# Five matrix products of a hybrid SSD and attention layer as seven block products for eight, the gates moved ahead of the scan

## The chip, the cores and the metric

One core of a Trainium2 chip runs the whole layer. The metric is the device time of one execution in microseconds: the kernel before took 2068.98 us (median of three runs, 2068.79 to 2068.99).

The engines are named as in the profile: PE (TensorE, matrix products; PEld its weight loads), DVE (VectorE), ACT (ScalarE), POOL (GpSimd), SP (the engine that issues most transfers). Each works through its own queue in order.

## The reference

A layer for 512 tokens of width 2048, in float32: a state space branch (SSD) and a latent attention branch side by side, gated, summed, projected, and normalised. Cut to what matters:

```python
h = rmsnorm(x, norm_w)
u = h @ w_in
z_ssm, xbc, dt_f, dt_b, q_a, kv_a, z_attn, g_ssm, g_attn = jnp.split(u, cuts, axis=-1)
xbc = silu(dwconv(xbc))                       # 4 taps over time
y = ssd_scan(...) + flip(ssd_scan(flip ...)) + d_skip * xs   # 32 heads of 64, 4 groups, chunks of 128
y = y.reshape(b, s, D_SSM) * silu(z_ssm)
y = rmsnorm(per group of 512)
q  = rmsnorm(q_a) @ w_uq ; kv = rmsnorm(kv_a) @ w_ukv        # 16 heads, rotary part of 64
o = bidir_attention(...) * silu(z_attn)
merged = sigmoid(g_ssm) * (y @ w_proj_ssm) + sigmoid(g_attn) * (o @ w_proj_attn)
x = x + merged @ w_out ; out = rmsnorm(x)
```

The products `h @ w_in` for z_ssm, g_ssm and g_attn and the two projections are each 512 x 2048 x 2048: the five products of the title.

## The kernel before, in words

**Products.** float32 operands are split into a high part rounded to PE's fp32r format and a low rest, and a product is three matmuls per 128 rows of depth (high x high, high x low, low x high). h is held transposed in `h_h` and `h_l` (16 tiles of depth by 512 tokens). Weights arrive from SP as chunks of 128x1024 (512 KB) into `wraw` (three buffers); ACT copies the chunk to `wh` (L153), DVE subtracts to `wl` (L154), and a chunk then feeds 24 matmuls: one result tile is 128 features by 512 tokens, two chunks, 48 matmuls in one PSUM bank (L158 to L160).

**Order of the work.** PE's instructions stand as the program writes them. A queue, `Fill`, holds generators of matmuls of weight products, and `gap()` takes a fixed number of them out between steps of the scan or of attention, so that PE has work while DVE, ACT and POOL prepare the next step. The other engines' orders are set by the scheduler at build time, by program order with a head start for weight loads and splits (`AHEAD = 60` instructions).

**Stages.** h is built; the tile of dt follows; then four groups of the scan (`ssd_group`). A group computes its six tiles of x, B and C (convolution rows L387 to L389, SiLU), transposes them (L424), and runs 18 pauses of 40 matmuls (4 tiles of z, 11 tiles of the gates silu(z_attn), sigmoid(g_ssm), sigmoid(g_attn), which go to DRAM). Between the pauses: weighted inputs `xw` on POOL (L483) and their split (L486, L487), local states `loc`, state updates, off-diagonal products; `yo` = D skip (L516, POOL); then for each of 4 chunks and 2 halves the decay sums (scan, L548), E (L551), G (L556 to L559) and the diagonal product `yb` (L569). z times y is normalised per group (sums of squares on PE, `rp`, L318) and stored, features by tokens. After the scan q and kv are compressed and rotary tables made, with the last four gate tiles as PE's cover; then 16 heads of attention (softmax on DVE and ACT; transposes of the probabilities L845), with the next heads' products and, in the last heads, the first projection's as filling. At the end the two projections (`wps` on y, `wpa` on o, 16 result tiles each), the gating and sum, and the output product (L997 to L999).

Of the kernel before, what the change touches and what calls it, by code (L numbers as in the profile page):

```python
# [18 lines left out]
P = 128  # L19
D = 2048  # L20
# [17 lines left out]
T_Z = T_XBC + 24  # L38
T_QA = T_Z + 16
T_KVA = T_QA + 6  # L40
T_ZA = T_KVA + 4
T_GS = T_ZA + 16
T_GA = T_GS + 16
N_TILES = T_GA + 16

# [28 lines left out]
Y_AHEAD = 4  # L74


def build(tc, a):
# [36 lines left out]
    zs_d = [dr.tile([P, SEQ], F32, name=f"zs_d{i}") for i in range(16)]  # L114
    gs_d = [dr.tile([P, SEQ], F32, name=f"gs_d{i}") for i in range(16)]
    ga_d = [dr.tile([P, SEQ], F32, name=f"ga_d{i}") for i in range(16)]
    y_d = [dr.tile([P, SEQ], F32, name=f"y_d{i}") for i in range(16)]
    o_d = [dr.tile([P, SEQ], F32, name=f"o_d{i}") for i in range(16)]
# [123 lines left out]
    sp = open_pool("sp", reuse_waits="tile")  # L242
    krp = open_pool("krp", side="right", reuse_waits="tile")
    kraw = krp.tile([P, SEQ], F32, name="kraw")
    dtp = in_gemm(T_DT, "dtp")
    kr_d = dr.tile([64, SEQ], F32, name="kr_d")
    act.copy(kraw[64:128, :], dtp[64:128, :])
    act.dma_start(kr_d, kraw[64:128, :])
    close_pool("krp")

    scn = sp.tile([P, 2 * SEQ], F32, name="scn")
    act.dma_start(scn, a["scn"])
    scan_f, scan_b = scn[:, :SEQ], scn[:, SEQ:]
    dsk = sp.tile([P, P], F32, name="dsk")[:, :NH]
    act.dma_start(dsk, a["dsk"].broadcast_to([P, NH]))

    dtT = sp.tile([P, TT, 64], F32, name="dtT")
    daT = sp.tile([P, TT, 64], F32, name="daT")
    da_d = dr.tile([64, SEQ], F32, name="da_d")
    ex = sp.tile([P, 2, 2, TT, NH], F32, name="ex")  # L260
    wst = sp.tile([P, 2, TT, NH], F32, name="wst")
    dec = sp.tile([P, TT, 64], F32, name="dec")


    dv_ = gp.tile([P, SEQ], F32, tag="st", bufs=3, name="dv_")
    dt64 = gp.tile([P, SEQ], F32, tag="st", bufs=3, name="dt64")
    act.activation(dv_[0:64, :], dtp[0:64, :], AF.Identity, bias=vec[0:64, V_DTB:V_DTB + 1])

    def dt_make(new):
# [23 lines left out]
        act.dma_start(da_d[NH:64, :], pl[NH:64, :])  # L293

# [57 lines left out]

    def gemm_steps(out, chunks, xh, xl):
# [10 lines left out]
    def gate_gen(tile_i, fn, dst):  # L364
        p_ = mm("gp")
        yield from gemm_steps(p_, win(tile_i), h_h, h_l)
        g_ = gp.tile([P, SEQ], F32, tag="st", bufs=3, name="gate")
        act.activation(g_, p_, fn)
        act.dma_start(dst, g_)

    gates = deque()
    for t0, fn, dst in ((T_ZA, AF.Silu, zs_d), (T_GS, AF.Sigmoid, gs_d), (T_GA, AF.Sigmoid, ga_d)):
        for i in range(16):
            gates.append((t0 + i, fn, dst[i]))
# [6 lines left out]

    def conv_silu(pst, ch, o):

        w = lambda k: vec[:, V_CW + ch * CW + k:V_CW + ch * CW + k + 1]
        acc = tmp2("cacc")
        act.activation(acc, pst, AF.Identity, bias=vec[:, V_CB + ch:V_CB + ch + 1], scale=w(2))
        dve.scalar_tensor_tensor(acc[:, 2:SEQ], pst[:, 0:SEQ - 2], w(0), acc[:, 2:SEQ], ALU.mult, ALU.add)  # L387
        dve.scalar_tensor_tensor(acc[:, 1:SEQ], pst[:, 0:SEQ - 1], w(1), acc[:, 1:SEQ], ALU.mult, ALU.add)
        dve.scalar_tensor_tensor(acc[:, 0:SEQ - 1], pst[:, 1:SEQ], w(3), acc[:, 0:SEQ - 1], ALU.mult, ALU.add)  # L389
        act.activation(o, acc, AF.Silu)  # L390
        return o
# [11 lines left out]
    def z_gen(g, ct, zs):  # L403
        p_ = mm("zp")
        yield from gemm_steps(p_, win(T_Z + 4 * g + ct), h_h, h_l)
        act.activation(zs[:, ct, :], p_, AF.Silu)

    pending = []

    def ssd_group(g):  # L410
# [27 lines left out]
        conv_silu(in_gemm(T_XBC + 6 * g + 4), 16 + g, BT)  # L438
        if g:
            pending.pop(0)()  # L440
        if g == 0:
            ahead[0] = AHEAD
            dt_make(tmp2)
        conv_silu(in_gemm(T_XBC + 6 * g + 5), 20 + g, CT)
        post_b()
        act.copy(c_h, CT)
        pool.tensor_sub(c_l, CT, c_h.bitcast(F32))
        prev = None
        for ct in range(4):
            xs = conv_silu(in_gemm(T_XBC + 6 * g + ct), 4 * g + ct, tmp2("xs"))  # L450
            if prev:
                prev()
            prev = post_x(ct, xs)
            if g == 0 and ct == 2:
                dt_turn()
            if g == 0 and ct == 3:
                dt_sums()

        zs = sw.tile([P, 4, SEQ], F32, tag="zs", name="zs")
        for ct in range(4):  # L460
            fill.add(("z", g, ct), z_gen(g, ct, zs))
        for _ in range(11):
            fill.add("gate", gate_gen(*gates.popleft()))
# [673 lines left out]
```

## Time and profile before

| what | number |
|---|---|
| median of the runs | 2068.98 us |
| the profiled execution | 2069.04 us, span 2067.3 us |
| start until the first transposes | 13 us |
| scan, four groups | about 55 to 1050 us, 249 us a group |
| compression, rotary tables | about 1050 to 1200 us |
| attention | about 1200 to 1515 us |
| projections | about 1515 to 1890 us |
| output product | about 1890 to 2067 us |

How to read the page: the header gives the span of the profiled execution; part 1 the busy time of each engine; part 2 the same in 40 slices in tenths, with the granted clock of PE and the transfer rates; part 4 the chain of work that ended last, by engine and by line; part 5 groups of instructions with busy time, mean duration of one and the idle time ahead of them with its releaser; part 6 the transfers with their median time to landing. The timeline lists single instructions: start, duration, engine, line, operation. The windows view gives for a stretch its length and the busy time of each engine in it.

### The profile page before, as it was taken

What the parts mean: (1) busy time and instruction counts of PE and PEld (TensorE: products, weight loads), DVE (VectorE), ACT (ScalarE), POOL (GpSimd) and SP (SyncE); (2) the same over time, 40 slices, a digit from 0 to 9 for tenths busy, and PEclk for the clock granted to TensorE, in tenths of its full rate; (3) what the DMA queues carried; (4) which work ended last, traced back from release to release, by engine and by line L of the source; (5) the groups of instructions that cost most, each with busy time, mean ns of one, the idle gap of its engine ahead of it and who ended that gap; (6) DMA issues with size and microseconds to landing.
All of it is one profiled execution on the core that took longest, in us unless ns stands there. A gap on an engine that the chain in (4) does not pass through costs nothing.

```text
span 2067.3 us, 24135 instructions
## 1 busy us (share of the span) xinstructions
PE 2035.6 (98%) x9498; PEld 1681.3 (81%) x9498; DVE 1122.7 (54%) x1531; ACT 791.2 (38%) x1103; POOL 189.8 (9%) x139
## 2 busy tenths in 40 slices
PE   6999999999999999999999999999999999999998
PEld 5888888888888888888788888888878888888886
DVE  4646755567545675447674657677663334343342
ACT  5433443334433354334433434444442222222232
POOL 1031000311003100111100000000011010000110
PEclk9999999999999999999999999999999999999999
DMA  5423443245332453224433333323345444335342
GB/s 186 124 82 116 155 131 112 87 128 162 121 108 83 148 153 122 92 90 150 138 122 103 105 119 88 102 81 98 102 123 168 145 150 134 122 119 182 104 141 81
DMA packets 116881, 252.16 MB, mean 122 GB/s; under 512 B 11168, under 2 KB 44064, under 8 KB 116768
## 3 DMA queue, kind: packets, MB, share of 16 engines
q1 hardware_dynamic: 101088, 222.33, 34.7%
q10 hardware_dynamic: 15680, 28.29, 3.7%
q8 instruction: 74, 1.21, 0.2%
q14 instruction: 39, 0.32, 0.0%
HBM read 220.96 MB, written 25.43 MB: 119 GB/s over the span
## 4 chain that ended last, share of the span: by engine, by line
PE 98%; DVE 1%; DMA 1%; ACT 0%; issue 0%; ACTq 0%
PE gp L158 8%; PE gp L159 8%; PE gp L160 8%; PE mm L160 6%; PE mm L158 6%; PE mm L159 6%; PE zp L158 3%; PE zp L160 3%; PE f L997 3%; PE zp L159 3%; PE f L998 3%; PE f L999 3%; PE pb L845 1%; PE qp L160 1%; PE qp L158 1%; PE qp L159 1%
## 5 line engine op out<-in xcount | busy, mean ns | idle before, releaser
L154 DVE TENSOR_TENSOR wl<-wraw,wh 128x1024 fp32r<-128x1024 f32 (+2 forms) x332 | 401.7, 1210 | 571.5 <-ACT wh L153 549.2
L153 ACT CAST wh<-wraw 128x1024 fp32r<-128x1024 f32 (+1 forms) x336 | 341.3, 1017 | 828.8 <-PE gp L159 214.1
L158 PE MATMUL gp<-h_h,wh 128*128 128x512 f32 x768 | 302.4, 394 | 0.0
L159 PE MATMUL gp<-h_l,wh 128*128 128x512 f32 x768 | 299.2, 390 | 0.0
L160 PE MATMUL gp<-h_h,wl 128*128 128x512 f32 x768 | 299.1, 390 | 0.0
L158 PE MATMUL mm<-h_h,wh 128*128 128x512 f32 x544 | 215.2, 396 | 0.0
L160 PE MATMUL mm<-h_h,wl 128*128 128x512 f32 x544 | 212.0, 390 | 0.0
L159 PE MATMUL mm<-h_l,wh 128*128 128x512 f32 x544 | 211.8, 389 | 0.0
L160 PEld LDWEIGHTS gp<-h_h,wl 128*128 128x128 f32 x768 | 144.2, 188 | 30.3
L158 PEld LDWEIGHTS gp<-h_h,wh 128*128 128x128 f32 x768 | 144.3, 188 | 29.9 <-issue 0.9
L159 PEld LDWEIGHTS gp<-h_l,wh 128*128 128x128 f32 x768 | 144.3, 188 | 29.3 <-issue 0.2
L159 PEld LDWEIGHTS mm<-h_l,wh 128*128 128x128 f32 x544 | 102.2, 188 | 22.0 <-issue 1.2
L158 PEld LDWEIGHTS mm<-h_h,wh 128*128 128x128 f32 x544 | 102.2, 188 | 21.8 <-issue 1.2
L160 PEld LDWEIGHTS mm<-h_h,wl 128*128 128x128 f32 x544 | 102.1, 188 | 21.5
L158 PE MATMUL zp<-h_h,wh 128*128 128x512 f32 x256 | 100.5, 392 | 0.0
L160 PE MATMUL zp<-h_h,wl 128*128 128x512 f32 x256 | 99.7, 389 | 0.0
L159 PE MATMUL zp<-h_l,wh 128*128 128x512 f32 x256 | 99.6, 389 | 0.0
L548 DVE TENSOR_TENSOR_SCAN sum<-da,scn 128x512 f32<-128x512 f32 x64 | 83.4, 1318 | 0.0
L997 PE MATMUL f<-wh,mh 128*128 128x512 f32 x208 | 80.9, 389 | 0.0
L998 PE MATMUL f<-wl,mh 128*128 128x512 f32 x208 | 80.9, 389 | 0.0
L999 PE MATMUL f<-wh,ml 128*128 128x512 f32 x208 | 80.9, 389 | 0.0
L835 ACT ACTIVATE pr<-s,nm 128x512 f32<-128x512 f32 x64 | 44.1, 689 | 79.7 <-DVE nm L833 78.2
(3625 smaller groups left out, 3715.0 us busy)
## 6 DMA issues: line engine op xcount, KB each, us to landing
wraw<-wi SPq DMA_DIRECT2D x198, 512.0 KB, 3.5
da<-da_d SPq DMA_DIRECT2D x64, 256.0 KB, 3.8
wraw<-wps SPq DMA_DIRECT2D x32, 512.0 KB, 3.5
wraw<-wpa SPq DMA_DIRECT2D x32, 512.0 KB, 3.7
wraw<-wo SPq DMA_DIRECT2D x32, 512.0 KB, 3.5
wraw<-wun SPq DMA_DIRECT2D x16, 384.0 KB, 3.0
xt<-x SPq DMA_DIRECT2D x8, 512.0 KB, 8.5
zs_d<-gate ACTq DMA_DIRECT2D x16, 256.0 KB, 2.9
```

What stands on the lines that cost most here:

```text
L153: act.copy(h, raw)
L154: (dve if ahead[0] else pool).tensor_sub(l, raw, h.bitcast(F32))
L158: pe.matmul(out, wh, xh, start=start, stop=False)
L159: pe.matmul(out, wh, xl, start=False, stop=False)
L160: pe.matmul(out, wl, xh, start=False, stop=stop)
L548: dve.tensor_tensor_scan(sums[dd], flat(da), mask, 0.0, ALU.add, ALU.mult)
L835: act.activation(pr, s, AF.Exp, bias=nm, scale=SCALE, accum_out=sm_)
L845: pe.transpose(tp[:, k * P:(k + 1) * P], prs[t][:, k * P:(k + 1) * P], ident)
L997: pe.matmul(acc, mh[:, tk], h[k], start=(kk == 0), stop=False)
L998: pe.matmul(acc, mh[:, tk], l[k], start=False, stop=False)
L999: pe.matmul(acc, ml[:, tk], h[k], start=False, stop=(kk == KT - 1))
```

## The change

**Seven for eight.** Each of the five products is cut into two halves of its columns (`cp`). A half is a 2 x 2 block product: tokens in two halves of 256, depth in two halves of 1024, columns in two blocks of 512. Instead of eight block products, seven are made of sums of blocks (Winograd's form, P1 to P7), each of 48 matmuls of 512 columns into two PSUM banks; the weights are now the moving operand, the result stands tokens by features, and a weight chunk feeds 12 matmuls instead of 24.

**Sums.** Of weight blocks: a transfer issued by POOL that adds a second block from DRAM into the chunk in place (`w_more`), and two DVE additions per chunk (`t2`, `t4`). Of result blocks: ACT evicts, DVE adds. Of h's blocks: DVE (`h_sums`), during the first xBC tiles; the block x21 of h is overwritten with S3 while the gates run and loaded back behind them. Of y's and o's blocks: transfers from DRAM to DRAM on POOL (copies and adding ones), then loads and splits like weights.

**Order.** Only group 0's xBC tiles come first; then z, sigmoid(g_ssm), sigmoid(g_attn) in full, to DRAM; then the scan, whose 18 pauses a group are filled with the next group's xBC tiles, the q and kv compression and silu(z_attn): 480 matmuls in the first three groups (27 or 26 to a pause), 576 in the last (32). y is normalised per 128 tokens on DVE and ACT (`y_norm`), transposed (`y_turn`) and stored. The normalisation of the compressed q and kv moves behind the scan, with 96 matmuls of silu(z_attn) left. In the last head three products of the first projection (`wps.head()`, 144 matmuls) are the filling; the operand blocks of y for the rest are loaded when the heads' memory is closed. `wpa`'s results get the first projection's by an adding transfer, and are transposed (64 more transposes) for the output product.

```diff
+    def w_more(t, w, cp, kh, cb, m, ahead_=AHEAD):
+        with tc.high_priority(offset=ahead_):
+            pool.dma_start(t, a[w][cp, kh, cb, m], accum_op=ALU.add)
...
+    def product(name, op, chunk, extra=None, pre=None):
+        bs = banks(name)
+        for m in range(4):
+            raw = chunk(m)
+            h, l = w_split(raw)
+            if extra:
+                extra(m, raw)
...
+            for i in range(2):
+                for jj in range(2):
+                    j = 2 * m + jj
+                    xh, xl = op(0, j, i), op(1, j, i)
+                    wh, wl = (t[:, jj * 512:(jj + 1) * 512] for t in (h, l))
+                    pe.matmul(bs[i], xh, wh, start=(j == 0), stop=False)
+                    pe.matmul(bs[i], xh, wl, start=False, stop=False)
+                    pe.matmul(bs[i], xl, wh, start=False, stop=(j == 7))
...
+                p1 = evict((yield from product("P1", self.op("x11"), c1, lambda m, raw: w_more(raw, w, cp, 0, 1, m))), "p1")
...
+            p5 = evict((yield from product("P5", self.op("S1"), c5, t2)), "p5")
...
+            A = yield from product("P6", self.op("S2"), lambda m: X[m],
...
+                yield from self.second(cp, p1, lambda i: p1[i], t4)
...
+            B = yield from product("P3", self.op("S4"), lambda m: Y[m], lambda m, raw: w_more(raw, w, cp, 0, 1, m),
...
+            A = yield from product("P7", self.op("S3"), lambda m: Y[m], None, self.pre(2, 2 * cp + 1))
...
+            A = yield from product("P4", self.op("x22"), lambda m: X[m], None, self.pre(2, 2 * cp))
...
+        left = [(10 * 48, 10 * 48, 10 * 48, 12 * 48)[g], 18]
...
+                y = sw.tile([P, SEQ], F32, tag="yz", bufs=2, name="y")
+                dve.tensor_add(y, yo[:, c], yb)
+                y_norm(c, g, y)
...
+    close_pool("at")
+    xb = cols = open_pool("xb", side="right", reuse_waits="tile")
+    for w in ("S1", "S2", "S4", "S3", "x22"):
+        y_ops.load(w)
+        y_ops.split(w, slot(w))
     fill.all()
...
+    run(wps.pair(0, True))
+    run(wps.pair(1, True))
+    sets[0] = list(range(4))
+    run(wpa.pair(0))
+    run(wpa.pair(1))
```

**Three places in the order.** On DVE at the first weights, before: the splits of the dt tile and group 0 stand among the rows of dt and of the convolution (`cacc`).

```order
L154 TENSOR_TENSOR wl<-wraw,wh 128x1024
L283 SCALAR_TENSOR_TENSOR pl<-pl,u 64x512
L284 SCALAR_TENSOR_TENSOR pl<-pl,e 64x512
L286 SCALAR_TENSOR_TENSOR dt_435<-pl,dv__434 64x512
L288 TENSOR_SCALAR da_518<-dt_435,small 64x512
L292 TENSOR_TENSOR pl<-dt_435,small 32x512
L387 SCALAR_TENSOR_TENSOR cacc<-mm,vec,cacc 128x510
```

Now, up to DVE's seventh weight split (the last row here), the sums of h's blocks (L651 to L671) and the splits of the sums (L421) stand with them:

```order
L666 TENSOR_TENSOR s_688<-x_686,x_678 128x1024
L282 SCALAR_TENSOR_TENSOR pl<-pl,e 64x512
L668 TENSOR_TENSOR x_686<-x_680,x_686 128x1024
L284 SCALAR_TENSOR_TENSOR dt_481<-pl,dv__480 64x512
L651 TENSOR_TENSOR x_694<-h_h,h_l 128x1024
L286 TENSOR_SCALAR da_489<-dt_481,small 64x512
L290 TENSOR_TENSOR pl<-dt_481,small 32x512
L377 SCALAR_TENSOR_TENSOR cacc<-xbc,vec,cacc 128x510
L421 TENSOR_TENSOR S_517<-x_686,S_517 128x1024
L378 SCALAR_TENSOR_TENSOR cacc<-xbc,vec,cacc 128x511
L162 TENSOR_TENSOR wl<-wraw,wh 128x1024
```

From DVE's first weight split to its seventh stand 26 operations of 128x1024, the splits included.

On POOL at the beginning of group 1 of the scan, before: behind the last G2 of group 0 come C's low part, two weighted inputs and the D skip.

```order
L557 TENSOR_TENSOR G_1950<-dtT,cbb 128x512
L557 TENSOR_TENSOR G_2036<-dtT,cbb 128x512
L557 TENSOR_TENSOR G_2124<-dtT,cbb 128x512
L447 TENSOR_TENSOR c_l<-CT,c_h 128x512
L483 TENSOR_TENSOR xw<-xT,wst 128x512 x2
L516 TENSOR_TENSOR yo<-xT,dsk 128x512 x4
```

Now, in group 2 (in groups 0 and 1 the same without the transfers):

```order
L832 TENSOR_TENSOR c_l<-CT,c_h 128x512
L1213 DMA yn_S_205<-yn_x_203 16x16384
L898 TENSOR_TENSOR yo<-xT,dsk 128x512 x4
L1216 DMA yn_S_207<-yn_x_203 512x512
L865 TENSOR_TENSOR xw<-xT,wst 128x512 x4
```

The D skip and the copies and sums of y's blocks went ahead of the first weighted input.

On DVE behind the last head's product with the values, before: `og` is the gated output of head 15, then operand splits of y alternate with the splits of weights.

```order
L859 TENSOR_TENSOR og<-op,zt 128x512
L867 TENSOR_TENSOR y11l<-y11st,y11h 128x512
L154 TENSOR_TENSOR wl<-wraw,wh 128x1024
L867 TENSOR_TENSOR y13l<-y13st,y13h 128x512
L867 TENSOR_TENSOR y15l<-y15st,y15h 128x512
L961 TENSOR_TENSOR ms_12445<-ps__12029,gt 128x512
```

Now (S_13035 to x_13071 are the operands S1, S2, S4, S3 and x22 of y; the `wl<-wraw` behind them belongs to the last chunk of the three early products, the `wl<-X` to P5):

```order
L1205 SCALAR_TENSOR_TENSOR og<-op,zt 128x512
L421 TENSOR_TENSOR S_13035<-xraw,S_13035 128x1024 x2
L424 SCALAR_TENSOR_TENSOR S_13044<-xraw,S_13044 128x1024 x2
L421 TENSOR_TENSOR S_13053<-xraw,S_13053 128x1024 x2
L421 TENSOR_TENSOR S_13062<-xraw,S_13062 128x1024 x2
L421 TENSOR_TENSOR x_13071<-xraw,x_13071 128x1024 x2
L421 TENSOR_TENSOR wl<-wraw,wh 128x1024
L421 TENSOR_TENSOR wl<-X,wh 128x1024 x2
```

Ten operand splits stand ahead of the weight split, where one stood.

More of the change, by code (lines that the diff above doesn't have):

```diff
@@ L351, in all, with run @@
                 self.step()
+    def run(gen):
+        for _ in gen:
+            pass
     def gemm_steps(out, chunks, xh, xl):
@@ L901, in build @@
             pv(hd - 1)
+        if hd == 12:
+            for step in sums(o_d, slice(0, 1024)):
+                for f in step:
+                    f()
         trans(hd, 0)
```

807 lines of the change are left out of this document (520 added, 287 removed).

## The prediction

> **What bounds the kernel now.** I read the page first: header, busy shares, clock row, chain by engine.
>
> ```profile
> span 2067.3 us, 24135 instructions
> PE 2035.6 (98%) x9498; PEld 1681.3 (81%) x9498; DVE 1122.7 (54%) x1531; ACT 791.2 (38%) x1103; POOL 189.8 (9%) x139
> ...
> PEclk9999999999999999999999999999999999999999
> ...
> GB/s 186 124 82 116 155 131 112 87 128 162 121 108 83 148 153 122 92 90 150 138 122 103 105 119 88 102 81 98 102 123 168 145 150 134 122 119 182 104 141 81
> ...
> PE 98%; DVE 1%; DMA 1%; ACT 0%; issue 0%; ACTq 0%
> ```
>
> TensorE (PE) carries 98% of the chain that ended last. The reader should see two things: every matmul less is worth its full step, and every microsecond in which PE waits in the new program is a loss, since hardly any waiting is left to absorb it. The timeline gives the step:
>
> ```profile
> 1799.65 0.39 PE L159 MATMUL pa__13946<-o4l,wh 128*128 128x512 f32 x1
> ...
> 1806.00 0.39 PE L160 MATMUL pa__13946<-o13h,wl 128*128 128x512 f32 x1
> ```
>
> From o4l to o13h/wl there are 28 matmuls in 6.35 us: 0.2268 us each (the 0.39 overlap).
>
> Next the load of VectorE (DVE) stage by stage, from the windows view: all of scan group 2, then two chunks inside the scan of group 1 (columns: window, length, PE, PEld, DVE, ACT, POOL busy, clock, DMA share, GB/s):
>
> ```profile
> 554.00:803.00 249.00, 249.00 (x1156) 203.46 (x1155) 145.96 (x167) 101.59 (x122) 33.86 (x25) 1.00 0.39 122
> 476.90:498.10 21.20, 21.20 (x107) 17.02 (x106) 15.52 (x20) 11.07 (x12) 2.35 (x2) 1.00 0.55 158
> 498.10:520.00 21.90, 21.90 (x111) 17.55 (x110) 17.24 (x22) 12.77 (x14) 2.36 (x2) 1.00 0.46 147
> ```
>
> The 54% on the page is an average: in a group DVE works 146 of 249 us, within the decay chunks 15.5 to 17.2 of 21 to 22 us. There PE never waits only because every pause of the scan is filled with 40 gate matmuls (9.07 us).
>
> **What is removed.** Two rows price transposes, one the sums of squares of y on PE:
>
> ```profile
> 109.98 0.60 PE L424 MATMUL pb<-cst,xs 128*128 128x128 f32 x4
> 110.42 1.06 PE L307 MATMUL pa<-daT,cst 128*128 128x128 f32 x8
> ```
> ```profile
> L318 PE MATMUL rp<-sq,cst 128*128 128x512 f32 x8 | 4.1, 590 | 0.0
> ```
>
> The five products take 3840 matmuls of 512 columns before (5 x 768) and 70 block products of 48 after, 3360: 480 x 0.2268 = 108.9 us less. Added are 64 transposes ahead of the output stage (four take 0.44 us, start to start: 7.0 us); the eight rp matmuls go (3.4 us, since two overlap). **PE work: -105 us.** I don't expect another step per matmul: the operands keep their 128x128 and 128x512 shapes.
>
> **The block products themselves.** These groups, by line and shape, price DVE, ScalarE (ACT) and GpSimd (POOL) work here and below:
>
> ```profile
> L154 DVE TENSOR_TENSOR wl<-wraw,wh 128x1024 fp32r<-128x1024 f32 x292 | 367.8, 1260 | 556.3 <-ACT wh L153 535.2 <-PE rp L318 16.8 <-PE pb L298 4.2
> L153 ACT CAST wh<-wraw 128x1024 fp32r<-128x1024 f32 x296 | 311.2, 1052 | 787.2 <-PE gp L159 209.3 <-PE mm L159 178.0 <-PE f L999 68.9
> L388 DVE SCALAR_TENSOR_TENSOR cacc<-mm,vec,cacc 128x511 f32<-128x511 f32 x24 | 18.0, 748 | 0.6
> L551 DVE TENSOR_TENSOR E<-sum 128x512 f32<-128x512 f32 x32 | 22.0, 686 | 0.4
> L180 DVE TENSOR_SCALAR rt<-rt 128x512 f32<-128x512 f32 x6 | 2.6, 427 | 0.2
> L178 DVE TENSOR_TENSOR small<-small 128x1 f32<-128x1 f32 x8 | 1.3, 159 | 0.3
> L177 DVE RECIPROCAL small<-small 128x1 f32<-128x1 f32 x8 | 1.3, 164 | 6.2 <-ACT small L175 6.2
> L552 ACT ACT_TABLE_LOAD x28 | 35.9, 1283 | 2.0 <-ACT gate L368 1.6
> ```
>
> Seven products run 7 x 48 x 0.2268 = 76.2 us on PE. DVE has 28 splits and 8 weight sums at 1.26 and 14 sums of results at 0.69: 55 us; ACT 28 casts at 1.05 and its evictions, 37 us; 20 loads of 512 KB are 138 GB/s, and the page's slices reach 186. So PE bounds this stage, unless the accumulating DMAs are late. Those are unseen: before issues no DMA on POOL. Nearest rows:
>
> ```profile
> wraw<-wi SPq DMA_DIRECT2D x198, 512.0 KB, 3.5
> xt<-x SPq DMA_DIRECT2D x8, 512.0 KB, 8.5
> zs_d<-gate ACTq DMA_DIRECT2D x16, 256.0 KB, 2.9
> ```
>
> A sum may start once its chunk has been split, some 3 us before PE uses it, and is wanted a product (10.9 us) later, less the 2.3 us of a cast and a split: slack about 11.4 us until PE waits. Bounds 3.5 and 8.5 us, both inside; I take 5, nearer to the 3.5 that 198 loads took; cost **0**. The 3 us of lead is an estimate; without it the slack is 8.4, and the upper bound would just reach it.
>
> The Trainium skill, page "DMA: Bandwidth & Descriptors", section "SWDGE vs HWDGE vs iDMA", has accumulating transfers only on the GpSimd path, where software writes the descriptors; its Measured table under "Bandwidth" gives such a load of 1 MB 6.15 us, so as an estimate some 3 us for 512 KB. No run here shows it; by that price the sum would be the same.
>
> **Where PE now waits.** *Start.*
>
> ```profile
> 31.78 0.47 PE L158 MATMUL dtp<-h_h,wh 128*128 128x512 f32 x1
> ```
> ```profile
> 35.42 0.74 DVE L220 SCALAR_TENSOR_TENSOR h_l<-pc,vec,h_h 128x512 fp32r<-128x512 f32 x1
> ```
> ```profile
> L283 DVE SCALAR_TENSOR_TENSOR pl<-pl,u 64x512 f32<-64x512 f32 x8 | 5.4, 681 | 0.2
> L278 DVE RECIPROCAL d<-d 64x512 f32<-64x512 f32 x1 | 3.3, 3334 | 0.0
> ```
>
> DVE issues in order; from its first weight split to the seventh stand 26 operations of 128x1024 (twenty of them block sums of h; 26 x 1.26 = 33 us), the dt chain (nineteen rows of 64x512 at 0.68, a reciprocal of 3.3: 16 us) and two convolution rows (1.5). DVE comes to the first at 36.1 us (35.42 + 0.68, h_l's end), so the seventh ends near 88; PE starts on the dt tile at 31.8 and, eight chunks of 24 matmuls (5.44 us each) later, wants it at 75.3. **12 us** (5 to 18).
>
> *First gate.* Overwriting h's x21 block with S3 waits for the last xBC matmul; a cast (1.05), two splits, three convolution rows and the next split stand ahead of P1: 1.05 + 2 x 1.26 + 3 x 0.75 + 1.26 = **7 us** (5 to 10).
>
> *Scan.* A pause is now 27 matmuls, 6.1 us. At a group's start before, POOL did xw first:
>
> ```profile
> 370.32 0.60 PE L424 MATMUL pb<-cst,xs 128*128 128x128 f32 x4
> 370.95 0.59 ACT L435 COPY xT<-pb 128x512 f32<-128x512 f32 x1 [3.69 <-PE pb L424]
> 371.67 2.05 POOL L483 TENSOR_TENSOR xw<-xT,wst 128x512 f32<-128x512 f32 x2 [46.37 <-ACT xT L435]
> 372.75 0.62 ACT L486 CAST xw_h<-xw 128x512 fp32r<-128x512 f32 x1 [1.21 <-POOL xw L483]
> 373.40 0.86 DVE L487 TENSOR_TENSOR xw_l<-xw,xw_h 128x512 fp32r<-128x512 f32 x1 [4.89 <-ACT xw_h L486]
> 373.68 5.94 POOL L516 TENSOR_TENSOR yo<-xT,dsk 128x512 f32<-128x512 f32 x4
> ...
> 380.33 0.39 PE L158 MATMUL loc<-xw_h,b_h 128*128 128x512 f32 x1
> ```
>
> xw_l was there at 374.3, loc needed it at 380.3. Now in groups 0 to 2 the four yo (5.94) come first: 0.65 + 5.94 + 1.0 + 0.65 + 0.86 = 9.1 us against 6.1, 3 us late; in group 2 two DRAM copies and sums also stand on POOL ahead, about 5 more (a put of 256 KB, 2.9 us by zs_d's row, and the issues, for which no row stands). Sum 14, less a little that other matmuls cover: 12 (6 to 18).
>
> Then the decay chunks. DVE per chunk: 16.4 (mean of the two windows) less 3.33 splits and two y rows (5.5), plus 2.25 splits (2.8), 1.1 tiles of convolution or squares (1.8) and the normalisation of y (two rows at 0.69, one 0.43, six 128x1 rows of 0.16: 2.75): 18.2 us. PE per chunk: 21.2 less 26 x 0.2268 = 15.3. DVE loses 2.9 us a chunk, and about 2 more where it waits for ACT's square root (a table load of 1.28 and 0.8 as in L177's idle time): 20 us a group. Three buffers of split weights allow it a lead of about 11 (two chunks of 5.44). Remainder 9 in each of groups 0 to 2; in group 3, with 32 matmuls a pause, nothing: 27 (0 to 60). **Scan 39 us.**
>
> *Scan to attention.* Behind the last y stand on DVE ten normalised tiles (10 x 1.43), some thirty rope rows at 0.43 to 0.75 (18), nine weight splits, and the eight of the query rope (5.5) until the value products' bank comes free: some 45 us, and about 8 until memory is free behind the last y and eleven tiles are loaded (two loads' time at 3.5, and the last y's own rows). PE has 96 matmuls of z left (21.8), the query rope's 36 (8.2) and a first value tile (3): **22 us** (10 to 35). Before, gate matmuls covered this.
>
> These windows show the busiest transfers and the clock:
>
> ```profile
> 0.00:35.00 35.00, 16.54 (x78) 14.39 (x79) 20.12 (x49) 24.45 (x43) 2.70 (x7) 1.00 0.57 209
> 1510.00:1515.00 5.00, 3.90 (x19) 2.69 (x18) 4.43 (x9) 2.39 (x6) 2.54 (x2) 1.00 0.73 210
> 1515.00:1520.00 5.00, 3.09 (x16) 1.99 (x14) 4.63 (x11) 3.61 (x9) 1.27 (x1) 1.00 0.71 193
> 1520.00:1530.00 10.00, 9.11 (x39) 7.55 (x40) 7.71 (x19) 6.07 (x13) 2.56 (x2) 0.83 0.60 171
> ```
>
> *Start of the projections.* The ten splits of y's operands (and, on SP, seven of their loads and eight weight loads) stand ahead of the split that the last 12 matmuls of the early products need, and their memory is free only after the last head. By DVE alone 10 x 1.26 + the head's own = 15 us; by the queue, sixteen loads of 0.52 MB and four sums are 10 MB, at the 209 to 210 GB/s that the busiest windows reached 50 us, of which the first three loads and what P5 doesn't need are early. Bounds 15 and 50; I take **26**, nearer to the first (18 to 40).
>
> *Small ones:* in the projections four splits of o's operands that stand ahead of a weight split (4 x 1.26 = 5), into the scan a cast and a split (2), ahead of the output stage the merged block's put and load, 2.9 and 3.5, half covered (3): **10** (3 to 20).
>
> *Clock.* Before lost its clock once, after its own wait at the last head (the last two windows above). Three idle microseconds in ten, then 0.83 for ten: 1.7 us. Six waits above are as long or longer (start, first gate, two in the scan, the two seams behind it): **10 us** (5 to 15).
>
> The Trainium skill, page "TensorE: Matmul & The Clock Gate", section "What's actually happening", says that the array falls to half its clock after an idle window of some 3.4 us and needs as long a busy one to return. By it the scan's waits of about 3 us would lose nothing, four waits would count, as an estimate 1.7 us each, and the sum would be 2087. The windows show a loss after idle pieces of 1.1 and 1.9 us, so the trace speaks for six.
>
> **The sum.** The profiled run took 2069.0 (span 2067.3 and 1.7 around it; median of the runs 2068.98). 2069 - 105 + 12 + 7 + 39 + 22 + 26 + 10 + 10 = **2090**. All waits at their low ends (52) give 2016, at their high ends (216) 2180.
>
> **Rivals.**
> *DVE leads in the scan.* If the scheduled order lets DVE run 20 us ahead of PE where a group's chunks begin, instead of 11, and xw is early, the 39 us go and some 6 of the clock's 10: 2045, faster. For it: DVE has spare time in a group's first half, and DVE's rows in a group sum to 115 to 122 us at these prices, under PE's 129. Against: weight splits wait for buffers that PE frees, and what stands behind them waits too. The point is a lead of 20 us.
> *Waits short everywhere* (loads early, low ends): 2016.
> *Late sums.* If an accumulating DMA takes over 11.4 us, PE waits twice in each of ten column halves: 20 us per microsecond over. At 13.5: 2069 - 105 + 42 and the 126 of waits: 2132. Against: even the slowest load of this size took 8.5.
> *Not what it says:* a product that ran over 0.26 us a matmul would save nothing; the shapes speak against it.
>
> **Chances.** Forecast (2075 to 2130) 0.50; DVE leads 0.20; short waits 0.16; late sums or waits at their high ends 0.13; the rest 0.01. The range 2010 to 2150 takes in the second and most of the third and fourth; the likeliest case alone has 2075 to 2130. What a measurement of this kernel can tell from no change is about 0.2%, 4 us. Faster (second and third case, and the rest) 0.37; slower (first and fourth, less 0.04 at their edges) 0.59; within 0.04.
>
> **What would show it.** Right: about 8900 matmuls, PE busy near 1930 us, no waits within the ten column halves; waits of PE on DVE in the scan (decay chunks 18 to 20 us each, DVE over 90%), one of 20 us on a split after the last head, one near 88 us from the start. Wrong: waits of PE on weight sums (then the DMAs were mispriced), scan groups under 135 us (DVE had the lead), or another step than 0.227 in the products.

## The result, and the profile after

The changed kernel takes 2230.2 us (median of four runs, 2225.2 to 2234.4) against 2068.9: 1.078 times as long, 95% interval 1.0756 to 1.0801. The sign was as forecast (slower), the size was not: 161 us more instead of 21, beyond the range.

The page of after, header, busy shares, clock, transfers and the chain by engine:

```profile
span 2228.7 us, 24606 instructions
PE 1996.5 (90%) x9074; PEld 1646.6 (74%) x9074; DVE 1458.4 (65%) x1938; ACT 960.0 (43%) x1335; POOL 269.7 (12%) x245
...
PEclk9999999999998998898999989999986999998999
DMA  5357655855535335535345733433558886977242
...
PE 66%; DVE 14%; DMA 9%; issue 7%; ACT 3%; POOL 1%; SPq 0%; ACTq 0%; DVEq 0%; POOLq 0%
```

The chain has gone from 98% PE to 66%. PE now idles 232 us of its span (2228.7 - 1996.5; before 2067.3 - 2035.6 = 32). Its busy time fell by 39 us only, though 105 us of matmuls went, so 66 us came in. The windows view over the 23 stretches in which the granted clock was half (82.1 to 89.0 is the first, 2038.0 to 2051.6 the last) accounts for most of it; this is its sum:

```profile
sum 208.20, PE 101.72 PEld 83.06 DVE 124.82 ACT 81.61 POOL 28.90; mean PE 4.42 PEld 3.61 DVE 5.43 ACT 3.55 POOL 1.26
```

PE was busy for 101.72 us in them, and four matmuls of 512 columns there take 1.70 us from start to start (695.96 to 697.66 in the timeline), 0.43 each instead of 0.227: 51 us lost. Of the other 15 us some 11 are, as an estimate, counting: a matmul ahead of a wait counts with 0.39 us instead of its step, and PE has some 70 gaps more than before. So 161 = -105 + 200 of waits + 51 of clock + 15.

Where, by the windows view (gates, scan, seam, heads, projections):

```profile
125.00:585.00 460.00, 459.53 (x2018) 379.93 (x2019) 314.81 (x304) 217.99 (x243) 41.39 (x48) 0.99 0.63 164
585.00:1240.00 655.00, 580.29 (x2630) 476.69 (x2628) 468.93 (x647) 298.79 (x434) 141.50 (x104) 0.94 0.45 143
1240.00:1340.00 100.00, 73.15 (x359) 62.15 (x360) 64.55 (x110) 36.82 (x63) 4.41 (x5) 0.86 0.58 162
1340.00:1661.00 321.00, 314.38 (x1623) 265.30 (x1623) 217.21 (x427) 142.12 (x275) 9.84 (x12) 0.99 0.44 128
1661.00:2046.00 385.00, 305.09 (x1305) 245.56 (x1303) 241.09 (x245) 152.52 (x163) 49.04 (x56) 0.91 0.80 217
```

Length, then PE's busy time: the gates run without a gap, 42 products in 460 us, 10.95 each. The scan idles 75 us at a clock of 0.94, the seam behind it 27 at 0.86, the projections 80 at 0.91, with the transfer engines 80% busy. Of the waits of PE by their releaser, the longest (total, times, longest one):

```profile
PE turn L785 <- DVE y L779: 55.6, 13, 10.8
PE P L524 <- ACT wh L420: 51.9, 6, 43.9
...
PE vp L1109 <- DVE qb L1079: 16.0, 1, 16.0
PE t L168 <- DVE wl L162: 10.7, 1, 10.7
PE P L525 <- DVE wl L421: 10.0, 11, 3.5
PE f L1383 <- ACT wh L420: 9.8, 1, 9.8
PE loc L167 <- DVE xw_l L869: 8.8, 5, 5.8
PE turn L1262 <- DMA p<-ms_d: 8.2, 2, 5.2
PE xbc L166 <- DVE cacc L379: 7.2, 1, 7.2
```

The reader is to see three things. The scan's waits are on `turn`, the transposes of the normalised y. One wait of 43.9 us stands at the start of the projections. And the waits are spread over more than twenty places, which matters for the clock. Around the first of the long waits in the scan the windows show it:

```profile
680.00:692.00 12.00, 1.36 (x6) 0.78 (x5) 11.79 (x21) 8.77 (x11) 0.00 (x0) 0.76 0.58 176
692.00:695.00 3.00, 2.95 (x15) 2.95 (x15) 0.00 (x0) 1.14 (x4) 0.00 (x0) 0.50 0.45 164
695.00:698.00 3.00, 3.00 (x9) 2.41 (x9) 2.66 (x4) 0.00 (x0) 2.09 (x2) 0.50 0.29 87
698.00:701.00 3.00, 3.00 (x10) 2.33 (x9) 3.00 (x4) 0.97 (x2) 1.24 (x1) 0.68 0.28 84
701.00:704.00 3.00, 3.00 (x17) 2.54 (x16) 3.00 (x4) 1.70 (x4) 0.00 (x0) 1.00 0.34 82
```

PE idles 10.7 us, works again from 692.0, and has half its clock until about 700: nine or ten instructions in 3 us where later 17 stand. Here the wait costs its own length and nearly 4 us behind it (9 us at a mean clock of 0.56). This is the dearest: by the same records the eleven other waits of over 5 us behind the start (84 us and later) were followed by 3.5 to 6.2 us at half clock, so each cost 1.7 to 3.1.

### The profile page after: what moved, and what is told of

Read it like the earlier page. It is cut to its first block, busy times and chain, and to the rows that moved or that the text cites. A ratio compares the mean times of both kernels' runs of the same rounds, so it can differ in the third digit from the quotient of the medians.

```text
span 2228.7 us, 24606 instructions
## 1 busy us (share of the span) xinstructions
PE 1996.5 (90%) x9074; PEld 1646.6 (74%) x9074; DVE 1458.4 (65%) x1938; ACT 960.0 (43%) x1335; POOL 269.7 (12%) x245
## 3 DMA queue, kind: packets, MB, share of 16 engines
q1 hardware_dynamic: 107568, 236.23, 32.7%
q0 software_dynamic: 19968, 65.02, 15.6%
## 4 chain that ended last, share of the span: by engine, by line
PE 66%; DVE 14%; DMA 9%; issue 7%; ACT 3%; POOL 1%; SPq 0%; ACTq 0%; DVEq 0%; POOLq 0%
PE P L525 9%; PE P L526 9%; PE P L524 9%; PE f L1384 2%; PE f L1385 2%; PE f L1383 2%; PE xbc L166 2%; PE xbc L167 2%; PE xbc L168 2%; DVE wl L162 2%; PE za L166 2%; PE za L167 2%; PE za L168 2%; DVE sum L930 2%; PE pb L1188 1%
## 5 line engine op out<-in xcount | busy, mean ns | idle before, releaser
L162 DVE TENSOR_TENSOR wl<-wraw,wh 128x1024 fp32r<-128x1024 f32 (+2 forms) x148 | 176.1, 1190 | 121.1 <-ACT wh L161 121.0
L421 DVE TENSOR_TENSOR wl<-X,wh 128x1024 fp32r<-128x1024 f32 x152 | 185.3, 1223 | 103.6 <-ACT wh L420 103.1
L420 ACT CAST wh<-X 128x1024 fp32r<-128x1024 f32 x152 | 159.1, 1053 | 178.2 <-PE P L526 135.2
L525 PE MATMUL P<-wl,S 128*128 128x512 f32 x544 | 215.4, 396 | 8.4 <-DVE wl L421 8.3
L524 PE MATMUL P<-wh,S 128*128 128x512 f32 x544 | 215.5, 396 | 2.5 <-ACT wh L420 2.5
L526 PE MATMUL P<-wh,S 128*128 128x512 f32 x544 | 214.2, 394 | 0.0
L166 PE MATMUL xbc<-h_h,wh 128*128 128x512 f32 x384 | 153.2, 399 | 7.2 <-DVE cacc L379 7.2
L421 DVE TENSOR_TENSOR wl<-wraw,wh 128x1024 fp32r<-128x1024 f32 x74 | 91.4, 1235 | 101.5 <-ACT wh L420 101.5
L421 DVE TENSOR_TENSOR wl<-Y,wh 128x1024 fp32r<-128x1024 f32 x80 | 97.9, 1224 | 89.9 <-ACT wh L420 89.8
L524 PE MATMUL P<-wh,h_h 128*128 128x512 f32 x384 | 150.4, 392 | 5.4 <-ACT wh L420 5.4
L167 PE MATMUL xbc<-h_l,wh 128*128 128x512 f32 x384 | 151.4, 394 | 0.0
L168 PE MATMUL xbc<-h_h,wl 128*128 128x512 f32 x384 | 151.2, 394 | 0.0
L524 PEld LDWEIGHTS P<-wh,S 128*128 128x128 f32 x544 | 104.0, 191 | 26.0 <-ACT wh L420 4.2
L526 PEld LDWEIGHTS P<-wh,S 128*128 128x128 f32 x544 | 103.7, 191 | 21.6
L524 PE MATMUL P<-wh,x 128*128 128x512 f32 x192 | 76.2, 397 | 43.9 <-ACT wh L420 43.9
```

Source lines behind the costliest of these rows:

```text
L162: (dve if ahead[0] else pool).tensor_sub(l, raw, h.bitcast(F32))
L166: pe.matmul(out, wh, xh, start=start, stop=False)
L167: pe.matmul(out, wh, xl, start=False, stop=False)
L168: pe.matmul(out, wl, xh, start=False, stop=stop)
L420: act.copy(hi_, raw)
L421: dve.tensor_sub(lo_, raw, hi_.bitcast(F32))
```

## The experiments

Times are compared with the changed kernel, 2230 us; its own runs differ by 9 us, so a difference under about 5 tells nothing. How much was gained where is read from the profiled execution of each run, and can differ from the medians by a few us.

**The scan: too early, a chain, or DVE's rate?** First what DVE did ahead of the wait at 692, from the timeline of after (start, duration):

```profile
680.99 0.67 DVE L954 TENSOR_TENSOR y<-yo,yb 128x512 f32<-128x512 f32 x1
...
685.18 0.68 DVE L775 TENSOR_TENSOR y<-y,z 128x512 f32<-128x512 f32 x1
...
689.35 0.14 DVE L778 TENSOR_SCALAR small<-small 128x1 f32<-128x1 f32 x1
...
690.55 0.15 DVE L185 RECIPROCAL rr<-rt 128x1 f32<-128x1 f32 x1
...
691.51 0.49 DVE L779 TENSOR_SCALAR y<-y,rr 128x512 f32<-128x512 f32 x1
```

These are five of the nine rows of one small chain on DVE (two steps on ACT stand between them), 11 us from first to last, on an engine busy without a gap (11.79 of 12 us): between them stand convolutions, decay sums and weight splits. The chain's first row already came some 6 us behind its product (`yb`, 674.9). Behind the wait DVE itself idles 3.3 us. Two readings fit: each step of the chain queues anew, or DVE is simply full.

*e1: transposes one pause later.*

```diff
-                if q and turns:
+                if not q and turns:
                     y_turn(*turns.popleft())
...
         gap()
+        y_turn(*turns.popleft())
         gap()
         diag(*last)
```

> The transposes of y (turn, L785) are placed one pause later; nothing else is changed. Theory 'too early' (PE asks for the normalised y of a chunk before DVE, in order, has come to it, and DVE catches up in the two pauses behind): the 55.6 us of waits of turn on DVE fall under 15, some 20 us of low clock go with them, time 2230 falls by 45 to 75. Rival 'DVE is full' (DVE's work per decay chunk is above PE's, so PE is late by the same amount whatever it asks for next): the waits move to the diagonal products or to weight splits, time falls by under 20.

Measured 2196.7 (2193.7 to 2199.9): 33 less, between the two. The waits of turn fell from 55.6 to 28.6 us; at the first chunk they were still 9.7, 5.8 and 5.8.

*e2: half of the scan's weight splits on POOL.*

```diff
-            (dve if ahead[0] else pool).tensor_sub(l, raw, h.bitcast(F32))
+            share[1] += 1
+            (dve if ahead[0] and not (share[0] and share[1] % 2) else pool).tensor_sub(l, raw, h.bitcast(F32))
```

> In the scan every second weight split goes from DVE to POOL: some 10 splits of 1.26 us, 12.6 us of DVE per group. Theory 'too early': turn still waits, time falls by under 20. Rival 'DVE is full': the waits of turn on DVE fall by about 10 us in each of the first three groups, with their low clock, time falls by 35 to 65. If POOL's queue holds the splits back (each 2.4 us and behind its waits for DVE), PE waits for wl on POOL and the time rises.

Measured 2266.1 (2264.2 to 2267.6): 36 more, and not by splits arriving late: turn's waits rose to 85.0 us. DVE did lose the splits, but its other rows grew. The groups by form within the scan, after (585 to 1240) and then e2 (585 to 1275):

```profile
L162 DVE TENSOR_TENSOR wl<-wraw,wh 128x1024 fp32r<-128x1024 f32 x85 | 114.2, 1344 | 90.2 <-ACT wh L161 90.0
L930 DVE TENSOR_TENSOR_SCAN sum<-da,scn 128x512 f32<-128x512 f32 x64 | 86.1, 1365 | 0.0
```
```profile
L164 POOL TENSOR_TENSOR wl<-wraw,wh 128x1024 fp32r<-128x1024 f32 x41 | 110.3, 2689 | 129.0 <-ACT wh L162 99.8 <-DVE rr L191 20.7 <-PE off L168 5.5
L932 DVE TENSOR_TENSOR_SCAN sum<-da,scn 128x512 f32<-128x512 f32 x64 | 110.1, 1740 | 0.0
L164 DVE TENSOR_TENSOR wl<-wraw,wh 128x1024 fp32r<-128x1024 f32 x43 | 53.5, 1243 | 49.8 <-ACT wh L162 49.7
```

The splits' 61 us that left DVE were partly paid back by the decay sums alone (24 us). Since the order on DVE changed too, this run doesn't decide the question.

*e6: no normalisation chain; e7: two taps less.* The one takes the chain and little work away, the other work and no chain.

```diff
-        act.activation(z, y, AF.Square, accum_out=s_)
-        dve.tensor_scalar(s_, s_, 1.0 / 512, EPS, ALU.mult, ALU.add)
-        dve.tensor_scalar_mul(y, y, rsqrt1(s_))
```

> Leaves out the normalisation of y (square and sum on ACT, the 128x1 chain, one 128x512 row on DVE, and the square root's table loads); y times z stays. Theory 'chain' (the wait of 10.7 us at a group's first transpose is the way through DVE's and ACT's queues that each step of the normalisation has to stand in again): the 55.6 us of waits of turn on DVE fall below 15, time falls by 45 to 75. Rival 'DVE rate': DVE is relieved of 1.8 us a chunk, 7 us a group: waits fall by 15 to 25, time by 15 to 35.

Measured 2170.2 (2168.4 to 2173.9): 60 less, turn's waits 14.1 us in three places.

```diff
+        if ch in (16, 20, 0, 1, 2, 3):
-        dve.scalar_tensor_tensor(acc[:, 2:SEQ], pst[:, 0:SEQ - 2], w(0), acc[:, 2:SEQ], ALU.mult, ALU.add)
-        dve.scalar_tensor_tensor(acc[:, 1:SEQ], pst[:, 0:SEQ - 1], w(1), acc[:, 1:SEQ], ALU.mult, ALU.add)
+            dve.scalar_tensor_tensor(acc[:, 2:SEQ], pst[:, 0:SEQ - 2], w(0), acc[:, 2:SEQ], ALU.mult, ALU.add)
+            dve.scalar_tensor_tensor(acc[:, 1:SEQ], pst[:, 0:SEQ - 1], w(1), acc[:, 1:SEQ], ALU.mult, ALU.add)
```

> Leaves out two of the four taps of the convolution in groups 1 to 3: two DVE rows of 0.74 us for each of 18 tiles, 8.9 us of DVE in each of the first three groups of the scan. The normalisation's chain stays. 'DVE rate': the waits of 10.7 us fall to 2 to 5 each, time falls by 20 to 40. 'Chain': they stay above 8, time falls by under 12.

Measured 2222.0 (2218.8 to 2224.7): 8 less; the three long waits went from 10.7 to 7.9, 8.1 and 8.4, turn's waits in all from 55.6 to 50.5. Nine microseconds of DVE per group bought under 3 of each long wait; the chain, with some 6 us of DVE per group and its steps on ACT, bought 60 in all. That points to the chain; the next run tests it with all the work left in.

*e15: transposes two pauses later than in the change.* The condition is `if q and len(turns) > 1`, with the same line at the group's end as e1.

> The transposes of y two pauses later than in the change (one later took 33 us off, leaving 28.6 us of waits of turn on DVE in six places). Theory 'chain': with three pauses for the normalisation's way through DVE's and ACT's queues the waits of turn fall under 10 us, time to 2165 to 2185. Rival 'DVE rate': the waits move to the diagonal products or splits and the time stays within 8 of 2197.

Measured 2184.9 (2180.8 to 2189.1): 45 less, with all the work in place. What is left of the waits in the scan:

```profile
PE turn L785 <- DVE y L779: 9.1, 6, 3.7
PE yb L951 <- DVE y L954: 4.5, 5, 2.4
PE qkv L168 <- DVE wl L162: 4.3, 5, 1.0
```

A little moved to the diagonal products (yb) and to weight splits (qkv), as the rival had it, 8.8 us where 46.5 went. The most of the scan's loss was where the transposes stood.

**The seam behind the scan.** *e5: 96 matmuls moved from group 3's pauses.*

```diff
-        for kind, n in ((("qkv", 4),), (("qkv", 4),), (("qkv", 2), ("za", 2)), (("za", 12),))[g]:
+        for kind, n in ((("qkv", 4),), (("qkv", 4),), (("qkv", 2), ("za", 2)), (("za", 10),))[g]:
...
-        left = [(10 * 48, 10 * 48, 10 * 48, 12 * 48)[g], 18]
+        left = [(10 * 48, 10 * 48, 10 * 48, 10 * 48)[g], 18]
```

> 96 matmuls (21.8 us) of silu(z_attn) move from the pauses of group 3 to the seam between scan and attention. Theory 'seam' (26.7 us of waits there, since DVE has some 45 us of normalising and rotary rows and PE 33 us of work): the waits on t and vp fall by 20 to 27, group 3, whose pauses fall from 32 to 27 matmuls, gains 5 to 15 of waits: time falls by 8 to 25. Rival 'work only moves': group 3 comes to wait like the groups ahead of it (17 to 20 us and clock), time within 6.

Measured 2219.3 (2213.9 to 2225.3): 11 less. The waits on t and vp are gone, one of 9.4 us on a split takes their place, and group 3 waits 6.1 and 2.7 where it had one wait of 2.8. The seam was a lack of cover, as predicted.

**The projections.** The wait of 43.9 us in after, as the transfers and DVE show it (SP issues, then DVE):

```profile
1672.15 13.52 SPq L431 DMA_DIRECT2D xraw<-yn_S  x5
1689.10 2.03 SPq L431 DMA_DIRECT2D xraw<-yn_x  x2
1695.40 0.33 SPq L451 DMA_DIRECT2D wraw<-wps  x1
```
```profile
1705.83 1.23 DVE L421 TENSOR_TENSOR wl<-wraw,wh 128x1024 fp32r<-128x1024 f32 x1 [5.42 <-ACT wh L420]
```

The chunk that PE wants is issued at 1695.4, behind a row of operand loads that take turns with it on three buffers, and split at 1705.8; from 1672 to the split the windows view gives the transfer engines' busy share as 1.0. Is it this place, or the amount of transfers?

*e3: the last 12 matmuls of the early products ahead of the last head's product with the values.*

```diff
-    fill.run(24)
+    fill.run(36)
     pv(AH - 1, pb)
```

> The last 12 matmuls of the three early products of wps are placed ahead of the last head's product with the values, so that their weight load and split no longer stand behind the operand blocks of y. Theory 'queue' (the 43.9 us wait is that one split behind ten others): P5 then needs only S1, X and X's sum, the wait falls to about 25, time falls by 15 to 25. Rival 'volume' (the wait is some 10 MB that all must pass at 250 to 290 GB/s): the wait stays at 38 to 46, on a split of X, time changes by under 6.

Measured 2227.6 (2225.5 to 2233.4): 3 less, within the noise. The wait fell to 27.1 us as 'queue' said, the time hardly, as 'volume' said: new waits of 4.3, 3.3 and several under 2 stand behind it.

*e3b: only S1 and S2 loaded there, the other operands during P5, P6 and P3.*

```diff
-    for w in ("S1", "S2", "S4", "S3", "x22"):
+    for w in ("S1", "S2"):
         y_ops.load(w)
...
-        (0, "P5"): [o_sums(0), L(o_ops, "x11")],
+        (0, "P5"): [L(y_ops, "S4"), C(y_ops, "S4"), o_sums(0), L(o_ops, "x11")],
```

(and S3 in the same way at P6, x22 at P3)

> Of the five operand blocks of y only S1 and S2 are loaded when the last head's memory is free; S4, S3 and x22 follow during P5, P6 and P3. Theory 'queue': four instead of ten splits and one instead of seven loads stand ahead of the weight split: wait 43.9 falls to about 20, time falls by 15 to 30, unless the later loads make PE wait for S4, S3 or x22. Rival 'volume': 3.1 MB less of some 10 MB: the wait falls by 10 to 12, time by 5 to 15.

Measured 2223.7 (2220.2 to 2228.1): 6.5 less, at the lower end, the ranges just overlapping; the wait fell to 22.7 us. Half of the wait went, and under a third of that half came out as time.

*e8: transposes of the merged blocks one product later* (`after(2, turn)`, and one more `product_done()` behind the last product).

> The transposes of the merged blocks in the last projection (14.2 us of waits of turn, mostly on the transfer that adds the first projection's block, landing in some 9 us) are placed one product later. Theory: these waits go, with 3 to 4 us of low clock each: time falls by 12 to 28. Rival: the waits sit on weights that are late anyway (the transfer engines are 80% busy there): under 5.

Measured 2239.3 (2237.3 to 2242.9): 9 more, against the theory. The waits on the adding transfer shrank, but a transpose then waited 10.4 us on ACT's copy of another (turned). This move is no remedy.

*e4: without the 84 adding transfers of weight blocks.*

```diff
     def w_more(t, w, cp, kh, cb, m, ahead_=AHEAD):
-        with tc.high_priority(offset=ahead_):
-            pool.dma_start(t, a[w][cp, kh, cb, m], accum_op=ALU.add)
+        pass
```

> Leaves out the 84 transfers that add a second weight block to a chunk (so products are made of wrong blocks); all matmuls, splits and DVE sums stay. Theory 'sums hidden' (in the gates they land in about 7 to 8 us, inside the slack of a product; only at the start of the projections do they share the transfer engines with 8 weight and 7 operand loads): the gates change by under 3 us, the wait of 43.9 by 0 to 12, time falls by 5 to 20. Rival 'sums starve PE': time falls by 40 or more, most of it between 1600 and 2050 us.

Measured 2200.8 (2196.5 to 2202.8): 29 less, between the two; all of it behind the last head (the wait of 43.9 fell to 35.0, and those on the merged blocks nearly went), nothing in the gates (PE is busy for 459.54 of 460 us, in after for 459.53).

**Together.** *e11 and e16* joined e1 (e16: e15 and e3), e3b, e5 and e8.

> Transposes of y one pause later, operands of y loaded as they are needed, 96 matmuls moved to the seam, transposes of the merged blocks one product later. If the four losses stand apart, the gains add: 33 + 6 + 11 + about 15 = 65, time near 2165. If one transfer or DVE limit lies under all of them, under 45.

> As the run before, with the transposes of y two pauses later and the early products' last 12 matmuls ahead of the last head's end. If waits at places (not rates) are what the change lost, 2135 to 2160. Still slower than before's 2068, since start, first gate, the y operands' transfers and the output stage's start keep some 100 us of waits and low clock. The rival, that DVE's rate in the scan is the limit, gives no less than 2165.

Measured 2195.2 (2190.2 to 2197.1) and 2181.3 (2177.7 to 2185.8): 35 and 49 less, both on the rival's side ('under 45', 'no less than 2165'). But both contain e8's move, which lost 9 alone. *e17* is e16 without e8's edit.

> Transposes of y two pauses later, early products' last 12 matmuls ahead, operands of y as needed, 96 matmuls at the seam; the transposes of the merged blocks as in the change. If the gains stand apart: 45 + 10 + 11 = 66 from 2230, time near 2163. If what the projections gain at one place they lose at the next (one limit of transfers under all): 2175 to 2190, the stretch from the last head to the output product as long as before, some 360 us.

Measured 2166.8 (2163.0 to 2172.3), 1.048 times before (1.0461 to 1.0502), near the 2163 of gains that stand apart. Their place speaks otherwise. Of the 66 us of its profiled execution some 62 (52 by e15 and e5 singly) were gained ahead of the projections' first wait; from there to the wait ahead of the output product e17 takes 368.6 us where after takes 374.9, and 2.7 of that are the 12 matmuls that moved ahead. So the scan's and the seam's gains add, and in the projections the rival's sign came true: the stretch is nearly as long as before, and what e3b alone gained there (361.2) is not found again. *e18* is e17 without the 84 adding transfers.

> As the run before, with the 84 adding transfers of weight blocks left out (products of wrong blocks). Theory 'volume and latency of the sums' (the projections wait for transfers at several places, and the sums are a part of that traffic whatever the order): another 25 to 35 off, in the projections alone, the gates unchanged. Rival 'places' (the sums only hurt where the operands of y collided with them): under 15, since those loads are now spread.

Measured 2108.5 (2107.0 to 2110.9): 58 less than e17, more than either theory gave, and again behind the last head. The windows from the projections' first wait to the wait ahead of the output product, of after, e4, e17 and e18:

```profile
1661.87:2036.73 374.86, 304.22 (x1301) 245.16 (x1300) 238.64 (x243) 149.25 (x159) 49.04 (x56) 0.91 0.80 217
```
```profile
1665.90:2002.24 336.34, 295.14 (x1300) 242.32 (x1300) 238.40 (x243) 149.53 (x159) 17.59 (x20) 0.93 0.60 185
```
```profile
1602.40:1971.02 368.62, 306.38 (x1289) 244.53 (x1288) 236.99 (x242) 146.98 (x158) 49.04 (x56) 0.92 0.81 219
```
```profile
1607.06:1917.09 310.03, 291.34 (x1289) 240.00 (x1288) 236.06 (x242) 146.97 (x158) 17.58 (x20) 0.97 0.65 199
```

Of e17 and e18: the same work on PE (1289 instructions) in 369 and in 310 us, with idle time of 62 and 19 us and a clock of 0.92 and 0.97. The four rows together show more: e17's moves shorten this stretch by 6 us with the sums in place, about as much as it varies where nothing in it was moved (368 to 375 in after, e1, e5 and e15), and by 26 without them. That speaks for the sums as the limit behind the single places. Other loads land later for the sums' sake (e17, then e18):

```profile
Y<-wpa SPq DMA_DIRECT2D x8, 512.0 KB, 7.7
```
```profile
Y<-wpa SPq DMA_DIRECT2D x8, 512.0 KB, 4.6
```

*e20: as e17, the projections' sums by plain loads and DVE.*

```diff
+        if w in ("wps", "wpa"):
+            more = w_load(w_tile("w"), w, cp, kh, cb, m)
+            with tc.high_priority(offset=ahead_):
+                dve.tensor_add(t, t, more)
+            return
```

> As e17, but in the two projections the 36 second weight blocks come as plain loads into a third buffer and DVE adds them (36 rows of some 1.2 us, beside DVE's 241 us of work in 385); the gates keep the adding transfers. The same bytes come from DRAM. Theory 'price of the adding form' (by the page's queue table an added byte takes 1.7 times as long on the transfer engines as a plain one, and the sums land in 8 to 10 us): time falls by 25 to 50, near 2130. Rival 'bytes' (the projections are limited by what must be read whatever the form): under 12. If the third buffers or DVE become the limit, it rises.

Measured 2155.5 (2148.0 to 2164.9), some 11 less than e17, with runs that spread over 17 us: under the 12 of the rival 'bytes'. About a fifth of the 58 us goes with the form, or more, since the plain loads take turns on the three buffers too and DVE has 36 rows more. What the rest is, the second blocks' bytes, these buffers or the sums' place between a split and the next product, no run tells apart. This is the fastest version that computes the layer, 1.044 times before (1.0405 to 1.0464); none beat the kernel before. Even e18, which leaves the sums out, is 40 us above it.

## Why the prediction was wrong

The forecast was 140 us short. The waits make up 84 of that: 36 in the scan, 44 in the projections and the rest in small amounts elsewhere. PE's longer busy time, 66 us where 10 were booked as clock, makes up the other 56. Three steps failed: the scan's waits had another cause than the one given, the projections' cost of the adding transfers was put at nothing, and the clock's losses were counted at six places.

**PE's work, -105 us: right.** The gates took 460 us for 42 products of a predicted 10.89 each (457), with PE without gaps.

**Adding transfers at no cost: right in the gates, wrong in the projections.** The argument looked at the transfers of one column half alone, and there it holds (medians of after):

```profile
X<-wz POOLq DMA_DIRECT2D x8, 512.0 KB, 8.2
...
Y<-wgs POOLq DMA_DIRECT2D x8, 512.0 KB, 6.4
...
X<-wpa POOLq DMA_DIRECT2D x8, 512.0 KB, 9.3
```

The 6.4 to 8.2 us in the gates were within the bounds (3.5 to 8.5), above the 5 taken, and inside the slack, which by the prediction's own figures is 11.6 (3 + 10.9 - 2.3), not 11.4. The estimate of 3 us, worked out from the Trainium skill's page "DMA: Bandwidth & Descriptors", section "Bandwidth", whose table says nothing of adding, lies far below what the adding form takes. In the projections operand loads, gate loads, and copies and sums of o's blocks share the engines, which rise from 63 to 80% busy; there leaving the sums out is worth 29 us in the change (e4) and 58 with the other moves made (e18 against e17). The prediction had no term for this.

**Start 12 and first gate 7: right in place, a little short.** PE waits 7.2 us until 84 (predicted 12, until about 88) and 5.4 until 125. DVE's crowded queue is behind the first, as predicted, but a convolution row ended it (cacc, L379) and not the seventh weight split; the second ended on ACT's cast.

**Scan, 39 us: the step that failed first.** The idle time was 75 us. The prediction had DVE lose 2.9 us per chunk by its rate and 2 more on ACT's square root, less a lead of 11. The chunks came out at 18 to 21 us, as predicted, but DVE was full only up to a group's first wait. The windows of group 0 over all its chunks and of two chunks behind that wait:

```profile
655.00:732.00 77.00, 62.53 (x286) 51.97 (x285) 68.81 (x101) 40.83 (x60) 14.29 (x9) 0.89 0.51 158
692.00:713.00 21.00, 19.20 (x81) 16.07 (x82) 16.42 (x25) 7.59 (x14) 3.33 (x2) 0.81 0.48 156
713.00:732.00 19.00, 16.97 (x83) 14.18 (x82) 15.71 (x25) 10.96 (x20) 4.89 (x3) 0.91 0.48 157
```

DVE works 16.4 and 15.7 us a chunk there (78 and 83% of the time), not 18.2 and over 90%. e7 shows that its rate is worth little (8 us for 27 us of work), and e6 and e15 that the way of a short chain through its queue was worth 45 to 60: nine rows, the first four behind work that had nothing to do with them, and a transpose that wanted the end of it one pause after the product that starts it. The amount fell inside the step's own bounds (6 to 78) by luck: they were drawn for another cause. Counting DVE's work against PE's per chunk can't see this; reading where the chain's steps stand in the order could have. The waits for xw came out at 11.6 us for a predicted 12 (8.8 on DVE's split and 2.8 on ACT's cast).

**Scan to attention, 22 us: right.** 26.7, on the predicted instructions (t 10.7, vp 16.0); e5 confirms the lack of cover. (DVE's rows as listed add up to 49 us, not 45, which comes nearer still.)

**Start of the projections, 26 us between bounds of 15 and 50: mis-sized.** 43.9 us. The transfers ended last, not DVE; the bound by the queue was the right one, and it was passed over for the nearer one.

**Small ones, 10 us: mis-sized.** The projections idle 80 us, so 36 beside the 43.9: some eleven waits on splits (10.0), the transposes of the merged blocks (14.2) and the output's first weight (9.8).

**Clock, 10 us: the largest error of a single term, 51 by the clock records (66 with what else lengthened PE's busy time).** That waits cost clock was right; the count was wrong. Six waits at 1.7 us each were booked, the latter from a single window of before; the trace has 23 stretches of half clock, 2.2 us each on the mean, some of them behind waits of only 1.0 (at 764) and 1.8 us (at 713). The Trainium skill's half clock, on its page "TensorE: Matmul & The Clock Gate", section "What's actually happening", is what the windows show. The busy stretch that this section wants before the full clock returns, some 3.4 us, was 7.9 us behind the wait at 692 and 3.5 to 6.2 behind the other long ones.

The rivals: DVE did not lead. The late sums came true in the projections only, not by a landing time over 11.4 us but by what they did to all other loads.

## What to carry to other kernels

Where one engine does 98% of the critical chain, removing 5% of its work only pays if everything that hid behind that work still hides; list each place where cover is taken away, and count a lost clock behind each wait on top of it (here 2.2 us on the mean). A wait that shrinks is not yet time gained: in the projections half of the longest one went and little came out, until the transfers behind it went too. A short chain of dependent steps on a nearly full engine that works in order can cost several times its own time (here 11 us for rows of under 3 on DVE), since a step may stand behind other work each time: place its consumer several pauses later before asking for less work. A transfer's cost is to be judged in the stage where the most other transfers run, not in the one where it is easiest to work out.

## What the runs showed of the hardware

- An adding transfer is dear for the transfer engines too. In part 3 of after's page POOL's queue, which issues all adding transfers and some copies, moved 65 MB for 15.6% of the engines' time, SP's 236 MB for 32.7%: 1.7 times as much per byte. In e4, without the 84 sums of weight blocks, POOL's queue moved 21.0 MB for 4.7%; by the difference the sums alone took 1.8 times as much per byte.

```profile
q1 hardware_dynamic: 107568, 236.23, 32.7%
q0 software_dynamic: 19968, 65.02, 15.6%
```

- POOL's work can slow DVE's. In e2, where POOL ran half of the scan's splits, the mean decay sum on DVE rose from 1365 to 1740 ns, and a 128x512 product on DVE took 2.70 us where it takes 0.7, while POOL ran a split of 2.80 us. Whether POOL was slowed in turn, these runs don't show.

```profile
680.16 2.70 DVE L943 TENSOR_TENSOR G<-G,E 128x512 f32<-128x512 f32 x1
```
```profile
679.51 2.80 POOL L164 TENSOR_TENSOR wl<-wraw,wh 128x1024 fp32r<-128x1024 f32 x1 [0.18 <-ACT wh L162]
```
